# Sums of squares of the first norm by matmuls with ones from the transposed input, and constants loaded behind the value weights

## The chip, the cores and the metric

The kernel runs on one core of a Trainium2 chip. The metric is the device time of one execution in microseconds (us). Before the change it is 1435.83 us, the median of three runs (1435.13 to 1435.89). The engines have short names: PE is the matrix engine, PEld its weight loads, DVE the vector engine, ACT the scalar engine, POOL the GpSimd engine, and SP the engine whose queue issues most DMAs. Each engine works its own queue in order.

## The reference

One decoder layer on x of 256 tokens by 2048 channels, all in float32, and a last norm. Cut to what matters:

```python
h = rmsnorm(x, norm1_g)                 # x * rsqrt(mean(x*x) + 1e-6) * g
proj = h @ w_in                         # columns: qkv, z, b, a, u, v, ga, gb
...                                     # qkv: causal conv, silu, l2norm, gated delta rule -> y_a
u = gelu(u_raw)
vg = layernorm(gelu(v_raw), sg_ln_g, sg_ln_b)
mixed = einsum(tril(sg_w), vg) + sg_b   # per group of 128 channels, over chunks of 128 tokens
y_b = u * mixed
merged = sigmoid(ga_raw) * (y_a @ w_branch_a) + sigmoid(gb_raw) * (y_b @ w_branch_b)
x = x + merged @ w_out
h2 = rmsnorm(x, norm2_g)
x = x + (silu(causal_dwconv(h2 @ ffn_w_gate) + b) * (h2 @ ffn_w_up)) @ ffn_w_down
return rmsnorm(x, final_norm_g)
```

## The kernel before

The weights stream through once. Every float32 product is made of three matmuls in a rounded format: a weight block is split into a rounded part `w_hi` (a cast on ACT, line 124) and the rest `w_lo` (a subtraction on DVE with two inputs in SBUF, line 127), the input likewise into `x_h`'s two halves, and PE multiplies hi by hi, hi by lo and lo by hi (lines 153 to 155). Raw weights have three slots of four rows of blocks (`wraw`), split ones four slots each of hi and lo (`wsp`), each for two k-blocks of 128 channels. So DVE's subtraction is on the way of every weight block to PE, and at most four split blocks can be ready ahead of PE.

The scale of the first norm is not applied to x before the products. `rstd1` (one number for each token, two columns for the two tiles of 128 tokens) scales the results when they are taken out of PSUM, where tokens lie on partitions; `rrow` (the same 256 numbers along the free axis, the same on all partitions) scales them where channels lie on partitions, in `chan_evict` (line 201, on POOL).

The order around the change:

- `vg_pass` (lines 296 to 321) multiplies x by the 1024 value columns. Its 16 k-blocks go in steps of one (the first four) or two; a step has two weight blocks, one for each half of the columns. The transposed x, `x_t`, comes in with the weights on SP's queue (lines 310 and 311), is scaled by `g1` and split (lines 209 and 210).
- At k-block 8, `tables` (lines 290 to 294) issues the loads of the constants `cst` and of x by rows, `xn`.
- Behind the pass SP's queue holds the loads of `par`, `ln_g`, `ln_b` (lines 324 to 326) and then the next weights.
- Line 328 squares `xn` on ACT, with a running sum along the row (`ss1`). `rsqrt_small` (lines 262 to 267) turns the sums into `rstd1`: DVE scales them and adds epsilon, POOL raises them to the power -0.5. `row_broadcast` (lines 269 to 278) makes `rrow`: DVE scales two identity matrices with `rstd1`, PE multiplies them by ones, ACT copies the result out of PSUM.
- Then come Gelu and the statistics of the value columns (lines 343 and 344), a second `rsqrt_small` for the layer norm (`sg_rs`), and the "bau" groups (lines 369 to 386), which multiply x by the columns of b, a and u: three groups of eight steps of two k-blocks. Between their steps the pieces of the layer norm are given to DVE, the first of which (line 355) needs `sg_rs` from POOL. After the first bau group POOL masks `ws` (line 389), PE transposes it.

The program gives this order, but a scheduler of the framework, working when the program is built, places each instruction in its engine's queue by when it takes it to be ready: in the trace the squares of line 328, for example, stand in ACT's queue between two casts of the value pass, ahead of work that the program has earlier.

Of the kernel before, what the change touches and what calls it, by code (L numbers as in the profile page):

```python
# [9 lines left out]
F32 = mybir.dt.float32  # L10
F32R = mybir.dt.float32r
AF = mybir.ActivationFunctionType
ALU = mybir.AluOpType
# [3 lines left out]
P = 128  # L17
D = 2048
T = 256
NT = T // P  # L20
NK = D // P
# [8 lines left out]
EPS = 1e-6  # L30
# [68 lines left out]
def decoder_kernel(ctx: ExitStack, tc: tile.TileContext, a: dict):  # L99
    nc = tc.nc  # L100
    out = a["out"]

    const = ctx.enter_context(tc.tile_pool(name="const", bufs=1))
# [5 lines left out]
    aux = ctx.enter_context(tc.tile_pool(name="aux", bufs=4, space=PSUM))  # L109

    def bank(pool, name):
        return pool.tile([P, 512], F32, name=name, tag="bank")
# [5 lines left out]
    def split(raw, shape, tag, dst=None, cast=None):  # L118

        hi, lo = dst or (  # L120
            wsp.tile(shape, F32R, name=f"w_{n}", tag=tag + n)[..., 0 : raw.shape[-1]] for n in ("hi", "lo")
        )
        if cast is None:
            nc.scalar.copy(hi, raw)  # L124
        else:
            cast.tensor_copy(hi, raw)
        nc.vector.tensor_tensor(lo, raw, f32(hi), op=ALU.subtract)  # L127
        return hi, lo

    def source(name, g):  # L130

        cols = GROUPS[name]
        return a["w_" + name], sum(n for _, n in cols[:g]), cols[g][1]
# [12 lines left out]
    def tok_mms(ps, x, n_k, k0, n, hi, lo):  # L146

        for t in range(NT):
            for j in range(n):
                k = k0 + j  # L150
                xh = x[:, k, t * P : (t + 1) * P]
                xl = x[:, k, T + t * P : T + (t + 1) * P]
                nc.tensor.matmul(ps[t], lhsT=xh, rhs=hi[:, j, :], start=(k == 0), stop=False)  # L153
                nc.tensor.matmul(ps[t], lhsT=xh, rhs=lo[:, j, :], start=False, stop=False)  # L154
                nc.tensor.matmul(ps[t], lhsT=xl, rhs=hi[:, j, :], start=False, stop=(k == n_k - 1))  # L155

    def tok_steps(x, src, n_k, name):

        ps = [bank(acc, f"{name}{t}")[:, 0 : src[2]] for t in range(NT)]
        for k0, n, hi, lo in stream(src, n_k):  # L160
            tok_mms(ps, x, n_k, k0, n, hi, lo)
            yield
        return ps

    def finish(steps):

        while True:
            try:
                next(steps)
            except StopIteration as e:  # L170
                return e.value
# [4 lines left out]
    def chan_group(x, src, name):  # L176


        ps = [bank(pool, name) for pool in (acc, acc, aux, aux)]
        for k0, n, hi, lo in stream(src, NK):  # L180
            for m in range(4):
                ms = slice(m * P, (m + 1) * P)
                for j in range(n):
                    k = k0 + j
                    xk = x[k // 8][:, k % 8, :] if isinstance(x, list) else x[:, k, :]
                    nc.tensor.matmul(  # L186
                        ps[m], lhsT=hi[:, j, ms], rhs=xk, start=(k == 0), stop=(k == NK - 1), skip_group_check=True
                    )
                    nc.tensor.matmul(  # L189
                        ps[m][:, 0:T], lhsT=lo[:, j, ms], rhs=xk[:, 0:T], start=False, stop=(k == NK - 1),  # L190
                        skip_group_check=True,
                    )
        return ps
# [9 lines left out]
    def split_stat(dst_hi, dst_lo, src, scale=None):  # L203

        if scale is None:
            nc.scalar.copy(dst_hi, src)
            nc.vector.tensor_tensor(dst_lo, src, f32(dst_hi), op=ALU.subtract)
        else:
            nc.scalar.activation(dst_hi, src, AF.Copy, scale=scale)
            nc.vector.scalar_tensor_tensor(  # L210
                dst_lo, src, scale, f32(dst_hi), op0=ALU.mult, op1=ALU.subtract
            )
# [21 lines left out]
    cst = const.tile([P, 128 * len(CONSTS) + 64 * len(CONSTS64)], F32, name="cst")  # L234
    cm = {n: cst[:, 128 * i : 128 * (i + 1)] for i, n in enumerate(CONSTS)}
# [3 lines left out]
    neg_half = const.tile([P, 2 * H], F32, name="neg_half")  # L239
    nc.gpsimd.memset(neg_half, -0.5)  # L240
    eps_t = const.tile([P, 1], F32, name="eps_t")
    nc.gpsimd.memset(eps_t, EPS)
    ss1 = const.tile([P, NT], F32, name="ss1")
    rstd1 = const.tile([P, NT], F32, name="rstd1")
    rrow = const.tile([P, T], F32, name="rrow")

# [3 lines left out]
    ln_b = sg.tile([P, SGW], F32, name="ln_b")  # L250
    ws = sg.tile([P, NG, P], F32, name="ws")
    x_ctx = ExitStack()
    xn = x_ctx.enter_context(tc.tile_pool(name="xn", bufs=1)).tile([P, NT, D], F32, name="xn")
    x_t = x_ctx.enter_context(tc.tile_pool(name="x_t", bufs=1)).tile([P, NK, T], F32, name="x_t")

    def bc(ap, axis, n):

# [4 lines left out]
    def rsqrt_small(dst, src, scale):  # L262

        n = src.shape[-1]
        v = small.tile([P, n], F32, name="rs_v", tag=f"rs_v{n}")
        nc.vector.tensor_scalar(v, src, scalar1=scale, scalar2=EPS, op0=ALU.mult, op1=ALU.add)
        nc.gpsimd.tensor_tensor(dst, v, neg_half[:, 0:n], op=ALU.pow)

    def row_broadcast(dst, col):

        ps = bank(aux, "ps_row")
        for t in range(NT):
            dg = small.tile([P, P], F32, name="dg", tag="dg")
            nc.vector.tensor_scalar(
                dg, cm["ident"], scalar1=col[:, t : t + 1], scalar2=None, op0=ALU.mult
            )
            nc.tensor.matmul(ps[:, t * P : (t + 1) * P], lhsT=cm["ones"], rhs=dg, start=True, stop=True)
        nc.scalar.copy(dst, ps[:, 0:T])
# [8 lines left out]
            dst[:, ks : ks + 4, t * P : (t + 1) * P], dst[:, ks : ks + 4, T + t * P : T + (t + 1) * P], pv  # L287
        )

    def tables():  # L290

        nc.sync.dma_start(cst, a["cst"])
        for t in range(NT):
            nc.sync.dma_start(xn[:, t], a["x"][t * P : (t + 1) * P, :])

    def vg_pass():

        ps = [[bank(pool, "ps_vg") for _ in range(NT)] for pool in (acc, aux)]
        for kb in range(0, NK, 4):
            raws = [wraw.tile([P, 4, 512], F32, name="w_raw", tag="raw") for _ in range(2)]  # L300
            n = 2 if kb else 1
            for j in range(0, 4, n):
                k0 = kb + j
                for c, raw in enumerate(raws):
                    at = P * 512 * (c * NK + kb)
                    block = a["w_vg"][at : at + P * 4 * 512].rearrange("(p k n) -> p k n", p=P, n=512)
                    if c == 0:
                        if k0 == 0:
                            nc.scalar.dma_start(g1, a["par"][:, 96:112])
                        nc.sync.dma_start(x_t[:, k0 : k0 + n, :], a["xt"][:, k0 : k0 + n, :])  # L310
                    nc.sync.dma_start(raw[:, j : j + n, :], block[:, j : j + n, :])
                if k0 == 0:
                    nc.scalar.copy(tbl, tbl)
                if k0 == 8:
                    tables()
                for k in range(k0, k0 + n):
                    split_stat(x_h[:, k, 0:T], x_h[:, k, T:], x_t[:, k, :], g1[:, k : k + 1])
                for c, raw in enumerate(raws):
                    hi, lo = split(raw[:, j : j + n, :], [P, n, 512], "w", cast=nc.vector if k0 + c == 0 else None)
                    tok_mms(ps[c], x_h, NK, k0, n, hi, lo)  # L320
        return ps

    ps_vg = vg_pass()
    nc.sync.dma_start(par, a["par"])
    nc.sync.dma_start(ln_g, a["sg_ln_g"].partition_broadcast(P))
    nc.sync.dma_start(ln_b, a["sg_ln_b"].partition_broadcast(P))
    for t in range(NT):
        nc.scalar.activation(xn[:, t], xn[:, t], AF.Square, accum_out=ss1[:, t : t + 1])
    x_ctx.close()
    rsqrt_small(rstd1, ss1, 1.0 / D)  # L330
    row_broadcast(rrow, rstd1)


    ba = const.tile([P, NT, 2 * H], F32, name="ba")
# [1 line left out]
    with sg_ctx:  # L336
# [32 lines left out]
        for c, (start, width) in enumerate(GROUPS["bau"]):  # L369
# [6 lines left out]
            ps = finish(steps)  # L376
# [415 lines left out]
    while True:  # L792
        try:
            n = next(main)
# [42 lines left out]
    for c in range(4):  # L837
        cs = slice(512 * c, 512 * (c + 1))
        ps = finish(wo_steps if c == 0 else tok_steps(x_m, source("out", c), NK, "ps_wo"))
        for t in range(NT):  # L840
            nc.vector.tensor_tensor(x2[:, t, cs], ps[t], x2[:, t, cs], op=ALU.add)
            sq = tmp.tile([P, 512], F32, name="x2_sq", tag="x2_sq")
            nc.scalar.activation(sq, x2[:, t, cs], AF.Square, accum_out=ss2[:, t, c : c + 1])
        for q in range(2):
            ps_t = bank(aux, "ps_x2t")
            for i in range(2):
                for t in range(NT):
                    k = 4 * c + 2 * q + i
# [3 lines left out]
            for i in range(2):  # L852
                k = 4 * c + 2 * q + i
# [4 lines left out]
    for f in range(0, NF, 2):  # L858
        ps = chan_group(x_h2, source("gu", f // 2), "ps_gu")
# [6 lines left out]
        for i in range(2):  # L866
# [8 lines left out]
            for j in range(2):  # L875
                nc.vector.scalar_tensor_tensor(
                    cv, gu[:, 0, 2 + j : 2 + j + T], fcw[:, 3 * ff + j : 3 * ff + j + 1], cv,
                    op0=ALU.mult, op1=ALU.add,
# [42 lines left out]
    for t in range(NT):  # L921
        for c in range(4):

            for h in range(1 if c < 3 else 2):
# [4 lines left out]
                sq = tmp.tile([P, 512], F32, name="x3_sq", tag="x2_sq")[:, 0:w]  # L929
# [79 lines left out]
```

## Time and profile before

The profiled execution took 1436.3 us (0.5 us above the median of the runs); its span from first to last instruction is 1434.5 us, at a mean granted PE clock of 0.997.

| engine | busy us | share of the span | instructions |
|---|---|---|---|
| PE | 1419.4 | 99% | 7776 |
| PEld | 1208.7 | 84% | 7776 |
| DVE | 896.0 | 62% | 1122 |
| ACT | 718.2 | 50% | 976 |
| POOL | 226.2 | 16% | 213 |

The DMA queues moved 269.19 MB, 188 GB/s on average; in the first fortieth of the span it was 305 GB/s. How to read the rows: a row of the timeline has the start in us, the duration in us, the engine, the line of the program, the operation, out <- in by the program's names, the shape (partitions x elements) and the count of instructions merged in the row; in brackets stands how long the engine had been idle just before and what ended the wait. A row of a group by source line has minimum, median and maximum duration in ns, then first and last start in us. A row of the waits has the total in us, the number of times, and the longest.

### The profile page before, as it was taken

What the parts mean: (1) busy time and instruction counts of PE and PEld (TensorE: products, weight loads), DVE (VectorE), ACT (ScalarE), POOL (GpSimd) and SP (SyncE); (2) the same over time, 40 slices, a digit from 0 to 9 for tenths busy, and PEclk for the clock granted to TensorE, in tenths of its full rate; (3) what the DMA queues carried; (4) which work ended last, traced back from release to release, by engine and by line L of the source; (5) the groups of instructions that cost most, each with busy time, mean ns of one, the idle gap of its engine ahead of it and who ended that gap; (6) DMA issues with size and microseconds to landing.
All of it is one profiled execution on the core that took longest, in us unless ns stands there. A gap on an engine that the chain in (4) does not pass through costs nothing.

```text
span 1434.5 us, 19535 instructions
## 1 busy us (share of the span) xinstructions
PE 1419.4 (99%) x7776; PEld 1208.7 (84%) x7776; DVE 896.0 (62%) x1122; ACT 718.2 (50%) x976; POOL 226.2 (16%) x213
## 2 busy tenths in 40 slices
PE   9999999999999999999999999999999999999997
PEld 7898888887888888888888888888888888888886
DVE  4756777779365644655566665766766666555555
ACT  5556556543433444445465554555545545444444
POOL 0001111221011200300031222322313221000002
PEclk9999999999999999999999999999999999999999
DMA  8764555445434455475555555555555555555552
GB/s 305 246 208 166 208 196 184 162 142 196 147 118 147 147 196 185 176 277 192 176 178 204 184 198 181 197 184 201 177 202 180 192 190 197 186 204 183 199 194 100
DMA packets 46907, 269.19 MB, mean 188 GB/s; under 512 B 4832, under 2 KB 12768, under 8 KB 16992
## 3 DMA queue, kind: packets, MB, share of 16 engines
q1 hardware_dynamic: 46384, 266.88, 52.9%
q8 instruction: 61, 1.00, 0.3%
q10 hardware_dynamic: 432, 1.06, 0.2%
q14 instruction: 30, 0.25, 0.1%
HBM read 265.83 MB, written 2.10 MB: 187 GB/s over the span
## 4 chain that ended last, share of the span: by engine, by line
PE 93%; DVE 3%; DMA 2%; POOL 1%; issue 1%; ACT 0%; SPq 0%; POOLq 0%; DVEq 0%; ACTq 0%
PE ps_gu L186 23%; PE ps_gu L189 11%; PE ps_qkv L186 6%; PE ps_dn L903 5%; PE ps_dn L901 5%; PE ps_dn L902 5%; PE ps_gate L153 4%; PE ps_gate L154 4%; PE ps_gate L155 3%; PE ps_qkv L189 3%; PE ps_wo L153 2%; PE ps_wo L155 2%; PE ps_wo L154 2%; PE ps_br L154 2%; PE ps_br L153 2%; PE ps_br L155 2%
## 5 line engine op out<-in xcount | busy, mean ns | idle before, releaser
L127 DVE TENSOR_TENSOR w_lo<-w_raw,w_hi 128x1024 fp32r<-128x1024 f32 (+3 forms) x412 | 530.0, 1290 | 359.3 <-ACT w_hi L124 357.1
L124 ACT CAST w_hi<-w_raw 128x1024 fp32r<-128x1024 f32 (+3 forms) x411 | 421.7, 1028 | 450.9 <-PE ps_gu L186 154.7
L186 PE MATMUL ps_gu<-x_h,w_hi 128*128 128x512 f32 x1408 | 488.5, 394 | 0.0
L189 PE MATMUL ps_gu<-x_h,w_lo 128*128 128x256 f32 x1408 | 390.3, 277 | 0.0
L186 PEld LDWEIGHTS ps_gu<-x_h,w_hi 128*128 128x128 f32 x1408 | 264.0, 187 | 61.0
L189 PEld LDWEIGHTS ps_gu<-x_h,w_lo 128*128 128x128 f32 x1408 | 264.4, 188 | 0.0
L127 DVE TENSOR_TENSOR w_lo<-wd_raw,w_hi 128x1024 fp32r<-128x1024 f32 x84 | 104.2, 1240 | 105.1 <-ACT w_hi L124 105.1
L124 ACT CAST w_hi<-wd_raw 128x1024 fp32r<-128x1024 f32 x84 | 88.6, 1055 | 120.2 <-PE ps_dn L903 113.0
L186 PE MATMUL ps_qkv<-x_h,w_hi 128*128 128x512 f32 x384 | 133.5, 394 | 0.0
L901 PE MATMUL ps_dn<-w_hi,y_s 128*128 128x512 f32 x336 | 130.7, 389 | 0.0
L903 PE MATMUL ps_dn<-w_hi,y_s 128*128 128x512 f32 x336 | 130.7, 389 | 0.0
L902 PE MATMUL ps_dn<-w_lo,y_s 128*128 128x512 f32 x336 | 130.7, 389 | 0.0
L201 POOL TENSOR_TENSOR gu<-gu,rrow 128x512 f32<-128x512 f32 x44 | 61.4, 1397 | 337.0 <-DVE gu L200 315.9
L189 PE MATMUL ps_qkv<-x_h,w_lo 128*128 128x256 f32 x384 | 106.5, 278 | 0.0
L153 PE MATMUL ps_gate<-w_hi,x_h 128*128 128x512 f32 x256 | 102.1, 399 | 0.0
L154 PE MATMUL ps_gate<-w_lo,x_h 128*128 128x512 f32 x256 | 100.0, 391 | 0.4 <-DVE w_lo L127 0.4
L155 PE MATMUL ps_gate<-w_hi,x_h 128*128 128x512 f32 x256 | 99.8, 390 | 0.0
L186 PEld LDWEIGHTS ps_qkv<-x_h,w_hi 128*128 128x128 f32 x384 | 72.0, 188 | 16.4
L902 PEld LDWEIGHTS ps_dn<-w_lo,y_s 128*128 128x128 f32 x336 | 63.1, 188 | 13.2
L903 PEld LDWEIGHTS ps_dn<-w_hi,y_s 128*128 128x128 f32 x336 | 63.1, 188 | 13.2
L901 PEld LDWEIGHTS ps_dn<-w_hi,y_s 128*128 128x128 f32 x336 | 63.1, 188 | 12.9
L189 PEld LDWEIGHTS ps_qkv<-x_h,w_lo 128*128 128x128 f32 x384 | 72.1, 188 | 0.1
(259 smaller groups left out, 1823.0 us busy)
## 6 DMA issues: line engine op xcount, KB each, us to landing
w_raw<-in_w_gu SPq DMA_DIRECT2D x88, 1024.0 KB, 4.8
wd_raw<-in_ffn_w_down SPq DMA_DIRECT2D x44, 1024.0 KB, 4.8
w_raw<-in_w_qkv SPq DMA_DIRECT2D x24, 1024.0 KB, 4.8
w_raw<-in_w_gb SPq DMA_DIRECT2D x16, 1024.0 KB, 4.8
w_raw<-in_w_ga SPq DMA_DIRECT2D x16, 1024.0 KB, 4.8
w_raw<-in_w_out SPq DMA_DIRECT2D x16, 1024.0 KB, 4.8
w_raw<-in_w_branch_b SPq DMA_DIRECT2D x8, 1024.0 KB, 4.8
w_raw<-in_w_z SPq DMA_DIRECT2D x8, 1024.0 KB, 4.8
```

Source lines behind the costliest of these rows:

```text
L124: nc.scalar.copy(hi, raw)
L127: nc.vector.tensor_tensor(lo, raw, f32(hi), op=ALU.subtract)
L153: nc.tensor.matmul(ps[t], lhsT=xh, rhs=hi[:, j, :], start=(k == 0), stop=False)
L154: nc.tensor.matmul(ps[t], lhsT=xh, rhs=lo[:, j, :], start=False, stop=False)
L155: nc.tensor.matmul(ps[t], lhsT=xl, rhs=hi[:, j, :], start=False, stop=(k == n_k - 1))
L186: nc.tensor.matmul(ps[m], lhsT=hi[:, j, ms], rhs=xk, start=(k == 0), stop=(k == NK - 1), skip_group_check=True)
L189: nc.tensor.matmul(ps[m][:, 0:T], lhsT=lo[:, j, ms], rhs=xk[:, 0:T], start=False, stop=(k == NK - 1), skip_group_check=True,)
L201: nc.gpsimd.tensor_tensor(dst, dst, bc(rrow, 1, 2), op=ALU.mult)
L901: nc.tensor.matmul(o, lhsT=yh, rhs=hi[:, cs], start=(k == 0), stop=False)
L902: nc.tensor.matmul(o, lhsT=yh, rhs=lo[:, cs], start=False, stop=False)
L903: nc.tensor.matmul(o, lhsT=yl, rhs=hi[:, cs], start=False, stop=(k == NF - 1))
```

## The change

`xn`, `ss1` and `tables` go. `cst` is loaded behind the value weights, ahead of `par`. In the value pass each pair of k-blocks of `x_t` is squared on ACT, and the squares are added up on DVE into `xss` (128 channels by 2 by 256 tokens; the first pair is squared straight into it). Behind the pass `norm1` sums over the channels by matmuls in float32: two with ones as the weights and `xss` as the moving operand, which give the row of 256 sums on all partitions, and four with `xss` as the weights and one column of ones, which give the two columns of sums. `rstd1` is made from the columns by `rsqrt_small` as before. `rrow` is made from the row: DVE scales it and adds epsilon, POOL raises 128 x 256 numbers to the power -0.5. `row_broadcast` is still used for the second norm.

```diff
-    xn = x_ctx.enter_context(tc.tile_pool(name="xn", bufs=1)).tile([P, NT, D], F32, name="xn")
-    x_t = x_ctx.enter_context(tc.tile_pool(name="x_t", bufs=1)).tile([P, NK, T], F32, name="x_t")
+    x_pool = x_ctx.enter_context(tc.tile_pool(name="x_t", bufs=1))
+    x_t = x_pool.tile([P, NK, T], F32, name="x_t")
+    xss = x_pool.tile([P, 2, T], F32, name="xss")
...
-    def tables():
-        nc.sync.dma_start(cst, a["cst"])
-        for t in range(NT):
-            nc.sync.dma_start(xn[:, t], a["x"][t * P : (t + 1) * P, :])
+    def square(k):
+        if k == 0:
+            nc.scalar.activation(xss, x_t[:, 0:2, :], AF.Square)
+        else:
+            sq = x_pool.tile([P, 2, T], F32, name="x_sq", tag="x_sq", bufs=2)
+            nc.scalar.activation(sq, x_t[:, k : k + 2, :], AF.Square)
+            nc.vector.tensor_tensor(xss, xss, sq, op=ALU.add)
+
+    def norm1():
+        ps = bank(aux, "ps_row")
+        for i in range(2):
+            nc.tensor.matmul(ps[:, 0:T], lhsT=cm["ones"], rhs=xss[:, i, :], start=i == 0, stop=i == 1)
+        for t in range(NT):
+            for i in range(2):
+                nc.tensor.matmul(
+                    ps[:, T + t : T + t + 1], lhsT=xss[:, i, t * P : (t + 1) * P], rhs=cm["ones"][:, 0:1],
+                    start=i == 0, stop=i == 1,
+                )
+        rsqrt_small(rstd1, ps[:, T : T + NT], 1.0 / D)
+        v = x_pool.tile([P, T], F32, name="rrow_v")
+        nc.vector.tensor_scalar(v, ps[:, 0:T], scalar1=1.0 / D, scalar2=EPS, op0=ALU.mult, op1=ALU.add)
+        nc.gpsimd.tensor_tensor(rrow, v, neg_half[:, 0:1].broadcast_to([P, T]), op=ALU.pow)
...
-                if k0 == 8:
-                    tables()
...
                     tok_mms(ps[c], x_h, NK, k0, n, hi, lo)
+                if n == 2 or j % 2:
+                    square(k0 + n - 2)
...
     ps_vg = vg_pass()
+    nc.sync.dma_start(cst, a["cst"])
     nc.sync.dma_start(par, a["par"])
     nc.sync.dma_start(ln_g, a["sg_ln_g"].partition_broadcast(P))
     nc.sync.dma_start(ln_b, a["sg_ln_b"].partition_broadcast(P))
-    for t in range(NT):
-        nc.scalar.activation(xn[:, t], xn[:, t], AF.Square, accum_out=ss1[:, t : t + 1])
+    norm1()
     x_ctx.close()
-    rsqrt_small(rstd1, ss1, 1.0 / D)
-    row_broadcast(rrow, rstd1)
```

More of the change, by code (lines that the diff above doesn't have):

```diff
@@ L242, in decoder_kernel @@
     nc.gpsimd.memset(eps_t, EPS)
-    ss1 = const.tile([P, NT], F32, name="ss1")
     rstd1 = const.tile([P, NT], F32, name="rstd1")
```

## The prediction

> **What bounds the kernel now.** I read the page first, then the waits of PE in the first 130 us, then the timelines of ACT and PE around the longest of them.
>
> ```profile
> span 1434.5 us, 19535 instructions
> PE 1419.4 (99%) x7776; PEld 1208.7 (84%) x7776; DVE 896.0 (62%) x1122; ACT 718.2 (50%) x976; POOL 226.2 (16%) x213
> ```
> ```profile
> PE ps_vg L153 <- ACT w_hi L124: 3.5, 1, 3.5
> ```
> ```profile
> 31.07 1.92 ACT L328 ACTIVATE xn<-xn 128x2048 f32<-128x2048 f32 x1 [2.57 <-DMA xn<-in_x]
> 33.58 1.91 ACT L328 ACTIVATE xn<-xn 128x2048 f32<-128x2048 f32 x1 [0.51 <-DMA xn<-in_x]
> 36.29 1.98 ACT L124 CAST w_hi<-w_raw 128x1024 fp32r<-128x1024 f32 x2
> ```
> ```profile
> 33.45 0.39 PE L155 MATMUL ps_vg<-w_hi,x_h 128*128 128x512 f32 x1
> 37.37 0.73 PE L153 MATMUL ps_vg<-w_hi,x_h 128*128 128x512 f32 x2 [3.53 <-ACT w_hi L124]
> 38.63 0.56 PE L154 MATMUL ps_vg<-w_lo,x_h 128*128 128x512 f32 x1 [0.53 <-DVE w_lo L127]
> 38.99 0.63 PE L155 MATMUL ps_vg<-w_hi,x_h 128*128 128x512 f32 x1
> 39.42 0.63 PE L153 MATMUL ps_vg<-w_hi,x_h 128*128 128x512 f32 x1
> 42.62 0.39 PE L153 MATMUL ps_vg<-w_hi,x_h 128*128 128x512 f32 x1
> 56.24 0.60 PE L277 MATMUL ps_row<-dg,cst 128*128 128x128 f32 x4
> 56.60 0.41 PE L153 MATMUL ps_u<-w_hi,x_h 128*128 128x348 f32 x1
> 57.17 0.32 PE L153 MATMUL ps_u<-w_hi,x_h 128*128 128x348 f32 x1
> 59.07 0.32 PE L153 MATMUL ps_u<-w_hi,x_h 128*128 128x348 f32 x1
> ```
> ```profile
> 38.50:42.50 4.00, 3.87 (x10) 0.57 0.70 215
> ```
>
> PE is busy 99% of the span, so a change counts by what it does to PE's few gaps. The value pass has the longest: ACT's queue holds the two squares of line 328 ahead of the next weight cast, and they wait for `xn`; the cast starts at 36.29 and PE stands from about 33.7 to 37.4. PE then works at a granted clock of 0.57 (fourth column of the windows row), a matmul every 0.43 us (38.99 to 39.42). From 42.62 to 56.24 sixty matmuls take 13.62 us, 0.227 each.
>
> **Part 1: `xn` and the squares by rows go.** Of the 192 matmuls of the pass 72 are left after 33.45 (two, ten more up to 42.62, sixty). Without the gap they take 72 x 0.227 = 16.3 us from 33.7 on, so the pass ends at 50.0 instead of 56.24: -6.2 us. What is late next? The weights of that step were in SBUF by 36.29, when the cast started without a wait for a DMA.
>
> ```profile
> 5.10:56.30 51.20, 46.84 (x196) 36.89 (x195) 28.37 (x41) 30.79 (x44) 0.85 (x3) 0.97 0.91 320
> 56.30:72.10 15.80, 15.80 (x103) 15.78 (x102) 15.16 (x25) 8.12 (x12) 2.54 (x2) 1.00 0.59 172
> ```
>
> The stage moved 320 GB/s, so the 2.1 MB of `xn` that no longer go ahead of these weights are worth 6.6 us: landed by 29.7, cast and subtracted some 2.3 us later, at 32.0, against 33.7 when PE wants them. The last three weight blocks are 1.5 MB behind, 5 us, and PE wants the first of them 8 us later. `cst` (0.69 MB, 2.2 us of that rate) goes behind them and delays `par`, `ln_g`, `ln_b` and the first bau weights in SP's queue by these 2.2 us, but it no longer goes ahead of half the value weights; its first reader is now at 50.0, over 10 us later than it would land. I count nothing for it; without that cover it costs its 2.2 us.
>
> **Part 2: squares from `x_t`.**
>
> ```profile
> L843 ACT ACTIVATE x_sq<-x x8: 614/620/630, 629.5 to 698.3; 128x512 f32<-128x512 f32 x8
> L364 DVE TENSOR_TENSOR vg<-vg,ln_g x4: 682/683/683, 63.7 to 70.5; 128x512 f32<-128x512 f32 x4
> ```
>
> Eight squares of that shape are 8 x 0.62 = 5.0 us of ACT (3.8 go), seven additions 7 x 0.68 = 4.8 us of DVE. In the stage of the first windows row above DVE is busy 28.4 and ACT 30.8 of 51.2 us, both with room, so PE's own work hides them: 0, at most 1.2 us if the first two squares each push back an early cast.
>
> **Part 3: the sums on PE.**
>
> ```profile
> 242.02 1.18 PE L520 MATMUL ps_g<-gl,cst 128*128 128x8 f32 x10
> 88.09 1.05 PE L404 MATMUL ps_mix<-vg,ws_t 128*128 128x128 f32 x8
> ```
>
> A float32 matmul has two records. Two of 256 columns: four records of twice 1.05 / 8, 1.05 us. Four of one column: eight records at the 0.12 of the 8-column ones, 0.94 us. Together 2.0 us, against 0.6 of `ps_row` before: +1.4, on PE's path. PE goes on to the bau groups at 52.0.
>
> **Part 4: the power on POOL.** POOL raises 2 numbers for `rstd1` as before, but now 256 columns for `rrow`. The trace has powers of 1, 2, 8 and 16 columns:
>
> ```profile
> L267 POOL TENSOR_TENSOR rstd<-rs_v,neg_half x2: 705/706/707, 36.0 to 699.5; 128x2 f32<-128x2 f32 x2
> L267 POOL TENSOR_TENSOR nrm<-rs_v,neg_half x2: 2912/2914/2915, 268.5 to 307.1; 128x16 f32<-128x16 f32 x2
> L267 POOL TENSOR_TENSOR o_rs<-rs_v,neg_half x2: 1637/2089/2541, 426.4 to 478.2; 128x8 f32<-128x8 f32 x2
> L267 POOL TENSOR_TENSOR r<-rs_v,neg_half x2: 551/553/555, 1419.4 to 1427.6; 128x1 f32<-128x1 f32 x2
> ```
>
> From 0.553 us for one column to 2.914 for 16 it is 0.157 us a column, and 2 and 8 lie on that line (0.71, 1.65). On it 256 columns take 0.55 + 255 x 0.157 = 40.7 us. That is far outside the measured shapes; the nearest other row is a multiplication of 512 columns, in 1.32 us (256.78, below), 0.0026 us a column. I take the line, since it is the same operation, and keep the multiplication as the other end.
>
> The Trainium skill's "GPSIMD Engine Reference", section "Elementwise — side-by-side cycle accounting", gives some 2.6 cycles at 1.2 GHz for each element of a two-input operation: an estimate of 0.55 us for 256 columns, with which the sum would be that of the first rival. The multiplications agree with it (2.6 ns), the powers don't (157 ns).
>
> Who waits? `norm1` ends at 52.0; scaling and the two-column power take about 1.6 us (0.7 by its row, the rest handing over and DVE being busy), so the long power runs from 53.6 to 94.3. POOL's queue has behind it the mask of `ws` and the power `sg_rs` of the layer norm, for which DVE waits:
>
> ```profile
> 57.05 1.26 POOL L389 TENSOR_SCALAR_AFFINE_SELECT ws<-ws 128x1024 f32<-128x1024 f32 x1 [20.39 <-DMA ws<-in_sg_w]
> 60.91 1.28 POOL L267 TENSOR_TENSOR sg_rs<-rs_v,neg_half 128x2 f32<-128x2 f32 x1 [2.60 <-DVE rs_v L266]
> ```
> ```profile
> 60.74 0.88 DVE L127 TENSOR_TENSOR w_lo<-w_raw,w_hi 128x696 fp32r<-128x696 f32 x1
> 62.23 1.54 DVE L355 TENSOR_SCALAR vg<-vg,mv,sg_rs 128x1024 f32<-128x1024 f32 x2 [0.60 <-POOL sg_rs L267]
> ```
>
> The long power's input is ready before Gelu has begun, so it goes first. And DVE is held before that:
>
> ```profile
> 256.78 1.32 POOL L544 TENSOR_TENSOR att<-g_df,cst 128x512 f32<-128x512 f32 x1
> 257.13 2.04 DVE L127 TENSOR_TENSOR w_lo<-w_raw,w_hi 128x1024 fp32r<-128x1024 f32 x1 [0.50 <-ACT w_hi L124]
> 267.14 1.23 DVE L127 TENSOR_TENSOR w_lo<-w_raw,w_hi 128x1024 fp32r<-128x1024 f32 x1
> ```
> ```profile
> 478.00 1.22 DVE L127 TENSOR_TENSOR w_lo<-w_raw,w_hi 128x1024 fp32r<-128x1024 f32 x1
> 478.17 2.54 POOL L267 TENSOR_TENSOR o_rs<-rs_v,neg_half 128x8 f32<-128x8 f32 x1 [2.90 <-DVE rs_v L266]
> ```
>
> The subtraction at 257.13 takes 2.04 us instead of 1.23: it ends 1.07 us after POOL does (258.10), so it was held until then. The power at 478.17 takes 2.54 instead of 1.64 and ends 1.5 us after the subtraction that was there first. The two take turns by whole instructions. So no `w_lo` is made from 53.6 to 94.3. Four split slots mean that at most four bau steps are ready by then; a step takes 1.90 us (57.17 to 59.07), and PE runs dry at 52.0 + 4 x 1.90 = 59.6. The fifth `w_lo` ends at 94.3 + 0.9 = 95.2. PE stands for 35.6 us, bounds 33 (five steps ready, the power from 53.0) and 39 (three, from 55).
>
> The skill's "SBUF — State Buffer", section "SBUF: two separate sides", says that the port which POOL and DVE share is held for the whole instruction, which no run here shows beyond 2 us. If the hold did not last, DVE would come as far as line 355 and wait there for `sg_rs`, with every later `w_lo` behind it: five steps, dry at 61.5, then 94.3 + 0.7 + 1.5 (line 355) + 0.7 (line 364) + 0.9 and up to 1.3 for the mask, resuming by 99: 1471.5 by the same sum as below.
>
> After the stop: ten matmuls at half speed cost 10 x 0.2 = 2 us, as after 37.37, and DVE, busy 15.16 of 15.80 us in the first bau group (second windows row) while it lives on its lead, has none left: 1 us, bounds 0 and 4. Later work only moves.
>
> **Sum**, against the profiled 1436.3: -6.2 + 1.4 + 35.6 + 3 = +33.8, 1470.1; the median of the runs is 0.5 lower: 1469.6 us.
>
> **Rivals.**
>
> 1. The power is cheap: it runs near the multiplication's 0.0026 us a column, 1.3 us at most, or anything up to 5 us (59.6 - 53.6 less a subtraction). POOL is done before PE runs dry, and only -6.2 + 1.4 is left: 1431.0. For it: POOL does 512 columns of other operations in 1.3 us. Against: four widths on one line. Faster, 9%.
> 2. The cost per column falls to half with width: 20.6 us, POOL done at 74.2, PE resuming at 75.1, a stop of 15.5: 1449.5. Nothing between 16 and 256 columns is in the trace: 5%.
> 3. The long power goes ahead of the two-column one. Then Gelu waits for `rstd1` with casts behind it on ACT, and PE resumes some 1.5 us later: 1471. Against: the two columns are scaled first. 4%.
> 4. The loads don't come early enough and the pass keeps its gap; the power starts 6 us later and all else with it: 1476. For it: the DMAs are 91% busy in the stage. 4%.
>
> The forecast with either form of DVE's wait has 78%. Its own range is 1460 to 1480: the bounds of the stop (-3, +3.5), of DVE's lead (-1, +3), of parts 1 and 2, and a slope 15% off (6 us). Rivals 3 and 4 lie in it too, and with 5% of the forecast's own outside it holds about 0.8; 1 and 2 are left out. About 0.2% (2.9 us) can be told from no change. Faster 0.09 (rival 1), the same 0.01, slower 0.90.
>
> **What would show it.** Right: no rows of `xn`; PE without a gap from 23 to 50 us; one POOL power row of 128x256 near 41 us, and no `w_lo` completed inside it; a PE wait of some 35 us in `ps_u` for DVE's `w_lo`; the clock low for 4 us behind it; from there the old profile, moved. Wrong: that POOL row at 1 us; `w_lo` rows inside it (no hold); `sg_rs` ahead of it.

## The result and the profile after

The changed kernel takes 1468.71 us (median of six runs, 1467.96 to 1469.25), the kernel before 1435.51 in the same comparison: a ratio of 1.0232, 95% interval 1.0219 to 1.0246. It is 33 us slower; the forecast was 1469.6, with a range of 1460 to 1480. The span of the profiled execution went from 1434.5 to 1466.7, by 32.2 us.

The first lines of the profile's page: PE is busy as long as before, POOL 40 us longer.

```profile
span 1466.7 us, 19565 instructions
PE 1420.0 (97%) x7784; PEld 1211.3 (83%) x7784; DVE 899.5 (61%) x1128; ACT 717.6 (49%) x979; POOL 266.1 (18%) x214
```

The waits of PE in the first 170 us (total, times, longest) answer to the 3.5 us wait of before. That one is gone, and one of 35.3 us is there:

```profile
PE ps_u L154 <- DVE w_lo L127: 35.3, 1, 35.3
PE ps_vg L153 <- DVE w_hi L126: 0.4, 1, 0.4
```

POOL's timeline has the power at once, line 313 of the changed kernel, between the two-column power ahead of it and what stands behind it, the mask of `ws` and `sg_rs`:

```profile
51.75 0.70 POOL L267 TENSOR_TENSOR rstd<-rs_v,neg_half 128x2 f32<-128x2 f32 x1 [50.69 <-DVE rs_v L266]
52.42 41.14 POOL L313 TENSOR_TENSOR rrow<-rrow_v,neg_half 128x256 f32<-128x256 f32 x1
93.52 1.10 POOL L406 TENSOR_SCALAR_AFFINE_SELECT ws<-ws 128x1024 f32<-128x1024 f32 x1
94.56 0.14 POOL L476 MEMSET pre<- 128x8 f32 x2
94.67 0.70 POOL L267 TENSOR_TENSOR sg_rs<-rs_v,neg_half 128x2 f32<-128x2 f32 x1
```

DVE's timeline shows who waited for `sg_rs`, and how:

```profile
55.70 0.83 DVE L127 TENSOR_TENSOR w_lo<-w_raw,w_hi 128x696 fp32r<-128x696 f32 x1
56.45 0.20 DVE L365 BATCH_NORM_AGGREGATE mv<-st 128x2 f32<-128x12 f32 x1
56.57 0.83 DVE L127 TENSOR_TENSOR w_lo<-w_raw,w_hi 128x696 fp32r<-128x696 f32 x1
57.31 0.16 DVE L266 TENSOR_SCALAR rs_v<-mv 128x2 f32<-128x2 f32 x1
95.40 1.54 DVE L372 TENSOR_SCALAR vg<-vg,mv,sg_rs 128x1024 f32<-128x1024 f32 x2 [37.92 <-POOL sg_rs L267]
96.85 0.69 DVE L381 TENSOR_TENSOR vg<-vg,ln_g 128x512 f32<-128x512 f32 x1
97.45 0.88 DVE L127 TENSOR_TENSOR w_lo<-w_raw,w_hi 128x696 fp32r<-128x696 f32 x1
```

Two things are to be read here. DVE stands for 37.92 us in front of one instruction of the layer norm (line 355 of before, 372 here), with the next `w_lo` behind it. And the two subtractions at 55.70 and 56.57 run while the power does, in 0.83 us each: this power did not keep them out.

PE's timeline, from the end of the value pass on:

```profile
49.59 1.02 PE L303 MATMUL ps_row<-xss,cst 128*128 128x256 f32 x4
50.45 0.95 PE L306 MATMUL ps_row<-cst,xss 128*128 128x1 f32 x8
51.26 0.41 PE L153 MATMUL ps_u<-w_hi,x_h 128*128 128x348 f32 x1
```
```profile
98.38 0.66 PE L154 MATMUL ps_u<-w_lo,x_h 128*128 128x348 f32 x1 [35.32 <-DVE w_lo L127]
98.84 0.49 PE L155 MATMUL ps_u<-w_hi,x_h 128*128 128x348 f32 x1
99.13 0.49 PE L153 MATMUL ps_u<-w_hi,x_h 128*128 128x348 f32 x1
```

The value pass ends at 49.59, before it was 56.24; the bau groups begin at 51.26, before 56.60. Six steps of them had their `w_lo` (two more than the four slots at one time, since PE frees slots as it goes), then PE stands until 98.38. The windows of PE's stop and of the time behind it (PE, PEld, DVE, ACT and POOL busy; then granted clock, DMA share, GB/s):

```profile
63.10:98.40 35.30, 0.02 (x1) 0.02 (x1) 3.00 (x5) 0.62 (x1) 32.26 (x5) 0.54 0.00 0
98.40:102.60 4.20, 4.20 (x14) 4.20 (x15) 4.20 (x7) 0.62 (x1) 0.00 (x0) 0.50 0.18 33
102.60:106.00 3.40, 3.40 (x24) 3.38 (x24) 3.40 (x7) 1.66 (x4) 0.00 (x0) 0.92 0.90 273
```

For 4.2 us behind the stop the clock is 0.50, a matmul every 0.29 us (98.84 to 99.13) instead of 0.16. What comes later has moved by about the same time. A good mark for that is the first row-scaled eviction of the qkv columns, before and after:

```profile
131.49 1.30 POOL L201 TENSOR_TENSOR pre<-pre,rrow 128x512 f32<-128x512 f32 x1 [5.42 <-DVE pre L200]
```
```profile
163.91 1.30 POOL L201 TENSOR_TENSOR pre<-pre,rrow 128x512 f32<-128x512 f32 x1 [5.42 <-DVE pre L200]
```

It has moved by 32.4 us, the span by 32.2. The experiments below are compared at this point too, called the mark. Two profiles of one kernel differ there by 0.3 us (`r1_identity` and `r1_again`) and by 0.6 us (`r2_power_late` and `r2_again`), so less than that is not told apart.

### The profile page after: what moved, and what is told of

Its sections match the earlier page's. It is cut to its first block, busy times and chain, and to the rows that moved or that the text cites. A ratio compares the mean times of both kernels' runs of the same rounds, so it can differ in the third digit from the quotient of the medians.

```text
span 1466.7 us, 19565 instructions
## 1 busy us (share of the span) xinstructions
PE 1420.0 (97%) x7784; PEld 1211.3 (83%) x7784; DVE 899.5 (61%) x1128; ACT 717.6 (49%) x979; POOL 266.1 (18%) x214
## 4 chain that ended last, share of the span: by engine, by line
PE 92%; issue 3%; DVE 3%; POOL 1%; DMA 0%; ACT 0%; POOLq 0%; DVEq 0%; SPq 0%
PE ps_gu L186 22%; PE ps_gu L189 11%; PE ps_qkv L186 6%; PE ps_dn L919 5%; PE ps_dn L920 5%; PE ps_dn L918 5%; PE ps_gate L153 4%; PE ps_gate L154 3%; PE ps_gate L155 3%; PE ps_qkv L189 3%; PE ps_wo L155 2%; PE ps_wo L154 2%; PE ps_wo L153 2%; PE ps_br L154 2%; PE ps_br L153 2%
```

## The experiments

The theories: **queue** (the long power stands ahead of the layer norm's power in POOL's queue, DVE waits in line for that one, PE for DVE), **hold** (as the prediction had it first: DVE cannot subtract while POOL takes the power), and **supply** (the sums from `x_t` themselves starve PE).

**The row scale by the identity again** (`r1_identity`), taken behind the first bau group and the transposes of `ws`, the power and the row matmuls gone:

```diff
     def norm1():
...
-        for i in range(2):
-            nc.tensor.matmul(ps[:, 0:T], lhsT=cm["ones"], rhs=xss[:, i, :], start=i == 0, stop=i == 1)
...
-        v = x_pool.tile([P, T], F32, name="rrow_v")
-        nc.vector.tensor_scalar(v, ps[:, 0:T], scalar1=1.0 / D, scalar2=EPS, op0=ALU.mult, op1=ALU.add)
-        nc.gpsimd.tensor_tensor(rrow, v, neg_half[:, 0:1].broadcast_to([P, T]), op=ALU.pow)
...
+                row_broadcast(rrow, rstd1)
```

> The changed kernel without the long power: the row scale is made from the two columns by the identity and ones, behind the first bau group, and the two row matmuls of norm 1 go. Theory: the 41 us power on POOL is the whole loss, so PE has no stop in the bau groups, keeps the shorter value pass (it ended at 49.6 instead of 56.2 us), and the time is near 1435.5 - 6.6 + 1 = 1430 us. Rival (the sums from the transposed x themselves starve DVE or ACT): a stop of several us stays in the value pass or the first bau group and the time is 1435 or more.

1431.68 us, 0.9963 of the kernel before (0.9951 to 0.9975). PE's waits on the value pass and the bau groups are down to this:

```profile
PE ps_vg L154 <- DVE w_lo L127: 0.3, 1, 0.3
```

The mark is at 126.68, 4.8 us earlier than before and 37.2 earlier than after. Supply falls: the squares and additions leave PE no wait over 0.3 us in the value pass, and what the sums still cost are 0.95 us of matmuls (eight records at 50.53). Without the long power the change gains, a little less than expected (1430). This version beats both kernels.

**The power kept, but later in POOL's queue** (`r2_power_late`). A column of epsilon, made from the mask of `ws` and from `sg_rs` times zero, makes the power wait for both:

```diff
-        nc.vector.tensor_scalar(v, ps[:, 0:T], scalar1=1.0 / D, scalar2=EPS, op0=ALU.mult, op1=ALU.add)
-        nc.gpsimd.tensor_tensor(rrow, v, neg_half[:, 0:1].broadcast_to([P, T]), op=ALU.pow)
...
+                nc.vector.tensor_scalar(
+                    eps_w[:, 0:1], ws[:, 0, 0:1], scalar1=0.0, scalar2=EPS, op0=ALU.mult, op1=ALU.add
+                )
+                nc.vector.scalar_tensor_tensor(
+                    eps_w[:, 1:2], rs[:, 0:1], 0.0, eps_w[:, 0:1], op0=ALU.mult, op1=ALU.add
+                )
+                nc.vector.tensor_scalar(
+                    rrow_v, ps_n1[:, 0:T], scalar1=1.0 / D, scalar2=eps_w[:, 1:2], op0=ALU.mult, op1=ALU.add
+                )
+                nc.gpsimd.tensor_tensor(rrow, rrow_v, neg_half[:, 0:1].broadcast_to([P, T]), op=ALU.pow)
```

> The changed kernel with its long power kept, but made to wait (through its epsilon) for the layer norm's power and the mask of ws, so that it stands behind both in POOL's queue. Queue theory (DVE waited in line for the layer norm's power behind the long one): no stop, about 1431 us, the power of 41 us runs beside the bau groups. Hold theory, as the prediction had it (DVE's subtractions cannot run while the power does): PE stops for some 35 us all the same, about 1468 us.

POOL's and DVE's timelines, then the group of the subtractions inside the power (71.4 to 118.6):

```profile
65.30 1.26 POOL L269 TENSOR_TENSOR sg_rs<-rs_v,neg_half 128x2 f32<-128x2 f32 x1 [10.64 <-DVE rs_v L268]
71.36 47.26 POOL L423 TENSOR_TENSOR rrow<-rrow_v,neg_half 128x256 f32<-128x256 f32 x1 [4.80 <-DVE rrow_v L420]
```
```profile
91.81 0.88 DVE L127 TENSOR_TENSOR w_lo<-w_raw,w_hi 128x692 fp32r<-128x692 f32 x1 [0.77 <-ACT w_hi L124]
```
```profile
L127 DVE TENSOR_TENSOR w_lo<-w_raw,w_hi 128x692 fp32r<-128x692 f32 x14 | 12.5, 905 | 5.9 <-ACT w_hi L124 5.9
L127 DVE TENSOR_TENSOR w_lo<-w_raw,w_hi 128x1024 fp32r<-128x1024 f32 x8 | 9.8, 1223 | 5.2 <-ACT w_hi L124 5.2
```

The same power, 22 subtractions inside it at their usual length, and no stop of PE: its longest wait for `w_lo` in the stage is 0.3 us. The mark is at 128.03, 3.5 us earlier than before. The hold falls, the queue stands. The power gets longer instead: 47.26 us beside a busy DVE, 41.14 beside one that was idle for most of it. That is 0.3 us for each subtraction; the power at 478.17 in the prediction grew by 0.9 us beside one, and why the two differ is open. The time of the whole kernel was less plain: 1435.85 us in the profiled execution, 1441.73 as the median of twelve runs (ratio 1.0016, 0.9998 to 1.0033; one run of 5058 us lies outside the ratio). So the stop is gone, but over all runs this kernel is not faster than the one before.

**A second look at it** (`r2_again`), the same kernel:

> The kernel of r2_power_late once more, for a second profile: its times lay at 1432 to 1436 and at 1441 to 1444 us. If the long power, which then ended at 118.6 us and took 47.3 us, varies in length, a run near 1442 us has it end some 10 us later, past 128 us, where the first row scale of the qkv columns waits for it, and PE stops there. If the power is as long as before, the difference lies elsewhere.

1441.78 us, with a power of 47.27 us that ends in time and a mark at 127.46, so the power is not what varies. The difference lies far behind it, in the gate and up groups of the feed-forward part: each of the 22 takes 22.61 us from one eviction to the next instead of 22.19, which makes 9.2 us. The two windows of 800 to 900 us, of the first execution and of the second:

```profile
800.00:900.00 100.00, 100.00 (x579) 88.19 (x578) 65.25 (x73) 53.14 (x74) 24.68 (x25) 1.00 0.54 190
```
```profile
800.00:900.00 100.00, 100.00 (x568) 86.76 (x567) 64.08 (x72) 51.62 (x72) 24.67 (x25) 1.00 0.53 187
```

PE is busy throughout and at full granted clock in both, with 579 and 568 matmuls. The qkv groups have two speeds as well. They ran at the slower one in the first execution of this kernel and in the profiles of `r5_constants_mid`, `r6_rows_behind` and `r1_again`, and at the faster one in `r2_again`; so the whole time differs by 5.9 us and not by 9.2. The times of all executions fit the four combinations, though only two were profiled: two near 1432.7 us, two near 1435.8, seven between 1441.4 and 1442.4, one at 1444.4. The two near 1432.7 come closest to the 1431 that the queue theory expected. Why there are two speeds was not found; gate and up groups at the slower one were seen in no other profile, so that something in this kernel favours it is not excluded. The mark, which lies ahead of most of these groups, tells more than the whole time where 1 to 3 us matter.

**Half of the power** (`r3_half_power`):

```diff
-        nc.gpsimd.tensor_tensor(rrow, v, neg_half[:, 0:1].broadcast_to([P, T]), op=ALU.pow)
+        nc.gpsimd.tensor_tensor(rrow[:, 0:P], v[:, 0:P], neg_half[:, 0:1].broadcast_to([P, P]), op=ALU.pow)
+        nc.vector.tensor_copy(rrow[:, P:T], v[:, P:T])
```

> The changed kernel with the power taken of 128 of the 256 columns; the other half of the row scale is left as the scaled sum, so the scale of the second token tile is left out where channels lie on partitions. By the line through 1, 2, 8 and 16 columns the power takes 0.55 + 127 x 0.157 = 20.5 us, PE's stop shrinks by 20.1 to about 15 us and the time is near 1448.6 us. If the long power has a large fixed part, the time stays near 1468.

```profile
52.91 20.74 POOL L313 TENSOR_TENSOR rrow<-rrow_v,neg_half 128x128 f32<-128x128 f32 x1
```
```profile
PE ps_u L154 <- DVE w_lo L127: 15.0, 1, 15.0
```

20.74 us against 20.5 expected, a stop of 15.0, 1449.14 us in the profiled execution and 1452.2 in the only other run, against 1448.6 expected. The line through 1, 2, 8 and 16 columns holds to 256: 41.14 - 20.74 = 20.40 us for 128 columns, 0.159 each.

**A long multiplication on POOL** (`r8_long_mult`, one run), to see whether another operation on POOL does hold DVE:

```diff
                 row_broadcast(rrow, rstd1)
+                lm = sg.tile([P, 4096], F32, name="lm_t")
+                nc.gpsimd.memset(lm, 1.0)
+                nc.gpsimd.tensor_tensor(lm, lm, rs[:, 0:1].broadcast_to([P, 4096]), op=ALU.mult)
```

> r1_identity with a multiplication of 128x4096 on POOL beside the first bau groups, about 10.5 us at 0.0026 us a column, whose result nothing reads. If a POOL instruction holds DVE's two-input subtractions for its whole length, one subtraction takes some 8 to 11 us instead of 0.88 and PE stops for some 3 to 6 us. If POOL gives way, as the 41 us power did, the subtractions keep 0.88 us and the multiplication gets longer.

```profile
58.41 7.01 POOL L412 TENSOR_TENSOR lm_t<-lm_t,sg_rs 128x4096 f32<-128x4096 f32 x1
```
```profile
58.37 8.33 DVE L367 TENSOR_SCALAR vg<-vg,mv,sg_rs 128x1024 f32<-128x1024 f32 x2 [0.83 <-POOL sg_rs L267]
66.62 0.68 DVE L376 TENSOR_TENSOR vg<-vg,ln_g 128x512 f32<-128x512 f32 x1
```

What was caught is the layer norm's pair of line 355 (367 here), not a subtraction: 8.33 us instead of 1.54, until 1.3 us after POOL's 7.01 us had ended. PE stopped for 5.5 us. So this multiplication kept the pair out for its whole length, as the one at 256.78 in the prediction kept a subtraction out; the long power kept none out. No run put the pair inside a power, or a subtraction inside a multiplication longer than 2 us, so that the operation on POOL alone decides it is argued from these cases, not shown. The Trainium skill's "SBUF — State Buffer", section "SBUF: two separate sides", which gives the first to reach the shared port the whole instruction, agrees with the multiplication and not with the power: the subtractions of 692 and 696 columns kept 0.83 to 0.91 us inside powers of 41.14 and 47.26 us.

**Where the gain in the value pass comes from** is asked by four smaller runs. First, x by rows loaded again, unused, on top of the best version (`r4_rows_loaded`):

```diff
+                if k0 == 8:
+                    for t in range(NT):
+                        nc.sync.dma_start(xn[:, t], a["x"][t * P : (t + 1) * P, :])
```

> r1_identity with x by rows loaded again at k-block 8, where the kernel before loads it, and not used by anything. If PE's stop of 3.5 us in the value pass came from the squares waiting in ACT's queue, the loads alone leave no stop and the time is that of r1_identity within 1 us. If it came from the 2.1 MB ahead of the weights, the weights of k-block 10 come some 6 us later, a stop of 2 to 4 us is back and the time is 3 to 6 us above r1_identity.

1433.12 us, mark at 128.32: 1.6 us later than without the loads, no wait of PE over 0.9 us. That lies between the two expectations, nearer the first: most of the old stop was the squares' place in ACT's queue while they waited for the rows, and the 2.1 MB themselves cost 1 to 2 us.

The constants at k-block 8 again, on top of the best version (`r5_constants_mid`; the `dma_start` of `cst` under `if k0 == 8`):

> r1_identity with the constants loaded at k-block 8 again, as in the kernel before. Theory: the 0.69 MB are hidden either way (the value pass is bound by PE), so the time is that of r1_identity, near 1431.7 us, within 1 us. Rival: the constants ahead of the weights cost their 2.2 us of transfer, 1434 us.

1433.16 us, but the mark at 126.77 against 126.68: without `xn` the constants' place makes no difference that can be seen. The whole time is of no use here, since the runs fall into two groups, near 1431.0 and 1433.5 us, and the profiled one had the slower qkv groups.

The kernel before with constants and `xn` loaded behind the value weights, and nothing else (`r6_rows_behind`):

```diff
-                if k0 == 8:
-                    tables()
...
     ps_vg = vg_pass()
+    tables()
```

> The kernel before with one edit: the loads of the constants and of x by rows stand behind the value weights; the sums are still made by rows on ACT, the row scale by the identity. If what was wrong before was only where the squares stood in ACT's queue, this has no stop in the value pass either, and the time is near 1431.5 us, with no sums from the transposed x at all. If the late rows delay Gelu and the casts behind it, PE stops for some us in the first bau group and the time is 1433 to 1438 us.

1435.02 us, ratio 0.9988 (0.9980 to 0.9997), mark at 129.11. The time is that of the second expectation, for another reason. The stop in the value pass is gone, and a smaller one stands at the start of the first bau group. ACT had ended the squares by 48.4 and then stood idle: its first cast there waits for the bau weights, whose load stands in SP's queue behind those of the constants and the rows.

```profile
PE ps_u L153 <- ACT w_hi L124: 1.9, 1, 1.9
```
```profile
46.37 1.92 ACT L327 ACTIVATE xn<-xn 128x2048 f32<-128x2048 f32 x1 [0.53 <-DMA xn<-in_x]
51.20 1.45 ACT L124 CAST w_hi<-w_raw 128x696 fp32r<-128x696 f32 x2 [2.82 <-DMA w_raw<-in_w_bau]
```

So here the 2.1 MB cost as traffic: in `r1_identity` the same cast starts at 46.98.

The kernel before with only the constants moved (`r7_constants_only`; the `dma_start` of `cst` taken out of `tables` and put behind the pass):

> The kernel before with only the constants moved behind the value weights; x by rows is loaded and squared as before. Theory: PE's stop in the value pass comes from the squares in ACT's queue, so it stays, only 1 to 2 us shorter if x by rows lands earlier by the constants' 2.2 us of transfer: 1434 to 1435.5 us. Rival: the constants ahead of the rows were what made the rows late, the stop goes and the time is near 1431 us.

1433.69 us, ratio 0.9981 (0.9972 to 0.9990), mark at 128.55. Neither was quite right: the squares still stand ahead of a cast, but the rows land earlier, the cast starts at 34.45 instead of 36.29 and PE's wait falls from 3.5 us to this:

```profile
31.74 1.92 ACT L328 ACTIVATE xn<-xn 128x2048 f32<-128x2048 f32 x1 [0.96 <-DMA xn<-in_x]
34.45 1.98 ACT L124 CAST w_hi<-w_raw 128x1024 fp32r<-128x1024 f32 x2
```
```profile
PE ps_vg L153 <- ACT w_hi L124: 0.8, 2, 0.7
```

Behind this wait the granted clock was 1.00 (36 to 38 us), where it was 0.57 behind the long one. So a cast that starts 1.8 us earlier let the pass end 3.4 us earlier (52.81 against 56.24), of which 2.9 are left at the mark.

The best version once more, on one chip with the last (`r1_again`):

> r1_identity once more, beside r7_constants_only on one chip: 0.9963 of the kernel before, as at first (1431.7 us), with no PE stop over 0.5 us in the first 100 us.

1433.51 us (ten runs, 1431.1 to 1434.46; the profiled one, 1434.21, had the slower qkv groups), ratio 0.9974 (0.9964 to 0.9983), mark at 127.00, no wait over 0.3 us. The expected time was met by the four runs up to 1431.72 only. Beside it on that chip `r7_constants_only`, which moves a single load, had 0.9981: the mark tells the two apart by 1.5 us, the whole times do not.

## Why the prediction was right, point by point

- **Part 1, the value pass.** -6.2 forecast, -6.65 measured (56.24 to 49.59); in the other profiles with this pass and no loads added it ended at 50.05 to 50.55. PE had no gap over 0.4 us there. That the squares, waiting in ACT's queue for the rows, were the cause is shown by `r4_rows_loaded` (rows loaded, no squares by rows) and `r6_rows_behind` (squares behind the pass): neither has the stop. That nothing is gained by the constants' place holds for the changed kernel; for the kernel before it is 2.9 us, since there they stood ahead of the rows for which ACT waited.
- **Part 2, squares and additions.** Hidden, as forecast: no wait over 0.3 us in `r1_identity`.
- **Part 3, the sums on PE.** 49.59 to 51.26, 1.67 us against 0.36 from the old row matmuls to the first of the bau groups: +1.3, forecast +1.4.
- **Part 4, the length of the power.** 40.7 forecast, 41.14 measured; its start 53.6 forecast, 52.42 measured.
- **Part 4, who waits.** Here the step "And DVE is held before that" failed. DVE was not held, and the two `w_lo` rows inside the power are the sign against a hold that the prediction had named; it came to the layer norm and waited in line, which is the second form that the prediction gave, for 1471.5 us. In that form five steps were to be ready, PE dry at 61.5 and back by 99; it was six, 63.06 and 98.38. The first form gave a stop of 35.6 us, the measured one is 35.3, by chance: the two steps more that ran are worth 3.8 us, and what stood between the end of the power and the next subtraction (the mask and `sg_rs` on POOL, then lines 372 and 381 on DVE, 93.56 to 97.45) took 3.9. What misled was the row at 478.17: a power that takes 0.9 us more beside a subtraction was read as turns by whole instructions; `r2_power_late`, whose power also got longer while 22 subtractions ran inside it, speaks for a power that is slowed and does not hold.
- **After the stop.** 3 forecast. The measured remainder is 32.2 + 6.65 - 1.3 - 35.3 = 2.2 us: the 0.50 clock over 4.2 us is 2.1 of it, so by this sum DVE's lost lead cost nearly nothing.
- **The rivals.** The cheap power would have been 1431.0 us; `r1_identity`, which has no long power, took 1431.68. The half price falls by the 41.14 us themselves and by `r3_half_power`. The two-column power went first (51.75), and the pass kept no gap, so the last two fall too.

## What to carry to other kernels

A cheap-looking instruction on an engine that is 16% busy can cost most of its length (here 35.3 of 41.1 us) if something with an early due time stands behind it in the queue: ask for each edit what is behind it, and price it by the same operation at other widths, not by another operation at the same width. Where a value is needed in two layouts, apply the costly function to the small layout and spread the result (here two columns, by the identity and ones) instead of applying it to the spread one. And a load costs by what waits for it in an in-order queue; the same 2 MB were worth 1 to 2 us as traffic and more as the thing that the squares ahead of a cast waited for. Moving the load that stood ahead of those rows (`r7_constants_only`) gave more than half of the gain at the mark without any new sums, so try the order of the loads first.

## What the runs showed of the hardware that was not expected

- A power on POOL takes 0.159 us a column of 128 partitions, 60 times the multiplications of 512 columns (0.0026), and did not keep DVE from its two-input subtractions; with 22 of them inside it got 6 us longer. The multiplication of 4096 columns by one broadcast column took 0.0017 us a column and did keep DVE out (one run).
- The groups with channels on partitions run at one of two speeds: 22.19 or 22.61 us for a gate or up group, 1.9% apart, at a granted clock of 1.00 in both. Within the two executions of `r2_power_late` and `r2_again` the speed stayed the same through all 22 of these groups.
